# The preparation's ARM tile in two buffers, with other step rates, in a two-layer hybrid backbone

## The chip, the cores and the metric

The kernel runs on one core of a Trainium2 chip. The metric is device time in microseconds (us) from one launch to its end, and the time of a kernel is the median over its runs. The core has a matrix engine (TensorE, PE here), a vector engine (VectorE, DVE), an activation engine (ScalarE, ACT), GpSimd (POOL) and SyncE (SP), which issues nearly all transfers. Each engine works through its own queue in order.

## The reference

1,024 latent tokens and 256 context tokens of width 1,024 go through two layers in float32. Each layer projects the normalised tokens once, splits the columns over four mixers (neighbourhood attention, multi-head latent attention, a bidirectional RWKV-7 recurrence, differential attention), concatenates, projects, and adds a gated MLP with a convolution. Cut to what matters here:

```python
for l in range(DEPTH):
    h_lat = rmsnorm(xl, norm1_g[l]) * (1.0 + sc1) + sh1          # h_ctx alike
    z_lat = jnp.split(h_lat @ w_in[l], IN_SPLITS, axis=-1)       # input projection
    na_l, na_c = na_mixer(z_lat[0], z_ctx[0], rpb[l], need_ctx)
    mla_l, mla_c = mla_mixer(z_lat[1], z_ctx[1], ...)            # low-rank q, k, v, rotary
    rk_l, rk_c = rwkv7_mixer(z_lat[2], z_ctx[2], ...)            # the recurrence
    df_l, df_c = diff_mixer(z_lat[3], z_ctx[3], ...)
    xl = xl + g1 * (jnp.concatenate([na_l, mla_l, rk_l, df_l], axis=-1) @ w_out[l])
    ...                                                          # conv-GLU

def step(S, inp):                                                # rwkv7_scan, per token and head
    r_t, w_t, k_t, v_t, a_t, b_t = inp
    sa = jnp.einsum('bhij,bhj->bhi', S, a_t)
    S = S * w_t[:, :, None, :] + sa[..., None] * b_t[:, :, None, :] + v_t[..., None] * k_t[:, :, None, :]
    return S, jnp.einsum('bhij,bhj->bhi', S, r_t)
```

## The kernel before

The recurrence is not run token by token. The 1,280 tokens are cut into ten slots of 128, and for each slot and direction the kernel prepares matrices with which 64 tokens are one step of a scan (20 steps a layer). That work is spread over the other mixers' work as follows.

In the dense phase of a layer, `main` computes the input projection in groups of six matmuls into a PSUM tile psd (three matmuls per product, of high and low halves: lines 140 to 142). It goes through the RWKV columns, the values, the MLA columns, then the differential and the neighbourhood queries and keys; layer 0 has 1,368 such matmuls. After every group `tick` hands out steps of the side generators: each generator has a rate, its account grows by the rate at each tick, and for every whole 1 in it the generator runs one step (up to its next `yield`) and so emits its instructions. A scheduler then orders each engine's queue by the order of emission and by its own simulation of when operands are ready. So the rates decide how far apart the side work stands in the queues.

- prep (`prep_gen`, lines 283 to about 520) does one slot after the other. partA: matmuls pu (line 333), decays and norms, POOL's kbc (line 368). partB: the tiles BK (DVE) and ARM (POOL, `arm`, lines 402 to 411: per slot four operations of 64x256 at line 407 and eight of 64x128 at line 410). PE multiplies them (`gram`, pg, line 440), ACT and DVE evict into NT, RB and back into ARM (`gout`, lines 446 to 448), PE transposes BK (pbt, line 460), and four transfers write NT, BT, RB and ARM to memory (rnt and rsg). ARM, BT, NT and RB have one buffer each. Slots 2 to 9 wait until the RWKV columns are complete.
- lanes (`lanes_gen`, line 526) inverts small triangular blocks of the slots that prep has written, in three groups: slots 0 and 1, 2 to 5, 6 to 9. A group is a load from rnt, 31 steps of a DVE product and a DVE reduce (lines 547, 548: tiles lpr, lXT, lM), twelve transfers out (lines 554, 557), reloads into the tiles G (lines 567 to 570), and matmuls pmg from G with evictions (lines 580, 582).
- mla (`mla_gen`, line 1390) starts when prep is done and the MLA columns are complete. It keeps its weight halves wq in prep's ARM tile, and its output tiles msp take turns in prep's BT and rwuwa tiles.

After the dense phase comes the attention: scores psL (line 803), softmax (reduces at DVE line 962, exponentials sm_P at ACT line 973), transposes psT, values psV. Beside it run the scan (`rw_step_gen`, line 603: pall at lines 664 and on, loads SG, VS and XB at lines 629 to 631, output tile yt), the modulation vectors (ada) and the recurrence's output stage. The scan's first step may start when the first lanes group is complete, and its later steps as theirs are. The pmg, pall and ada matmuls share one PSUM buffer (tag "R"), so they run in the order in which they are emitted. The yt tile lies in the pool rl, open for the whole mixer.

Of the kernel before, what the change touches and what calls it, by code (L numbers as in the profile page):

```python
# [9 lines left out]
F32 = mybir.dt.float32  # L10
F32R = mybir.dt.float32r
# [6 lines left out]
P = 128  # L18
# [22 lines left out]
class K:  # L41
# [241 lines left out]
    def prep_gen(self, l, rw, pool, psA, psB, F):  # L283
# [111 lines left out]
        def partB(sl):  # L395
            q = st[sl]
            z, kkm, ld, ta, L, E2, kd = (q[k] for k in ("z", "kkm", "ld", "ta", "L", "E2", "kd"))
            Wc = self.Wc[:, sl]
            BK = pool.tile([P, 2, 4, 3, 64], F32, tag="BK", name="BK", bufs=1)
            ARM = pool.tile([P, 2, 2, 4, 2, 64], F32, tag="ARM", name="ARM", bufs=1)  # L400

            def arm(d):
                for e in range(2):
                    r = slice(64 * e, 64 * e + 64)
                    for sl_, a, f in ((0, kkm, ld), (1, z[:, 0], E2)):
                        if d == 0:
                            GT(out=ARM[r, d, e, :, sl_], in0=v4(a)[r], in1=u4(f)[r, d], op=ALU.mult)  # L407
                        else:
# [18 lines left out]
            BKf = BK.rearrange("p d c s t -> p d c (s t)")  # L427
            ARf = ARM.rearrange("p d e c s t -> p d e c (s t)")
            BT = pool.tile([P, 2, 2, 4, 64], F32, tag="BT", name="BT", bufs=1)
# [960 lines left out]
    def mla_gen(self, l, rp, base, pp, ptag, pq, qtag):  # L1390
# [3 lines left out]
        flip = iter(range(10 ** 6))  # L1394

        def big(tag, shape, name, w, dt=F32):
            t = rp.tile([P, w], dt, tag=tag, name=name, bufs=2 if tag in ("sz", "ld", "E2") else 1)
            k = 1
            for x in shape:
                k *= x  # L1400
            t = t[:, :k]
            if len(shape) == 2:
                t = t.rearrange("p (a b) -> p a b", b=shape[1])
            return t
        mv = base.tile([P, 4], F32, name="mlav")
        nc.sync.dma_start(mv, A["mlv"][l])
        U = self.wunits()
        wq = big("ARM", (2, 768), "mwq", 2048, F32R)
        U.add(A["w_uq"][l], 768, lambda: (wq[:, 0], wq[:, 1]))
        U.add(A["w_ukv"][l], 512, lambda: (big("NT", (512,), "mwk", 512, F32R), big("RB", (512,), "mwl", 512, F32R)))  # L1410
        U.dma_to(1)
# [21 lines left out]
            TT(out=tv, in0=tv, in1=rt, op=ALU.add)  # L1433

        def out(t, dst, o):
            sp = big(("BT", "rwuwa")[next(flip) % 2], (2, 512), "msp", 1024, F32R)

            def f1():
                ACT(sp[0:96, 0], t[0:96], AF.Copy)

            def f2():
                TT(out=sp[0:96, 1], in0=t[0:96], in1=sp[0:96, 0].bitcast(F32), op=ALU.subtract)
                for h in range(2):
                    nc.sync.dma_start(dst[h, :, :, o:o + n].rearrange("w r t -> r w t"), sp[0:96, :, h * n:h * n + n].bitcast(F32))
            self.defer(f1, f2)
# [6 lines left out]
        for i, o in enumerate(todo):  # L1452
# [13 lines left out]
            for b in range(nb):  # L1466
                w = slice(b * P, (b + 1) * P)
# [20 lines left out]
            for hp in range(2):  # L1488
# [5 lines left out]
                t = big("ld", (512,), "mt", 512)  # L1494
# [9 lines left out]
                t = big("ld", (512,), "mt", 512)  # L1504
# [5 lines left out]
            for b in range(nb):  # L1510
                w = slice(b * P, (b + 1) * P)
# [119 lines left out]
    def mix(self, l, H, hclose, ada):  # L1631
        nc, A = self.nc, self.A
        need_ctx = l == 0
# [3 lines left out]
        rl, rlclose = self.open("rwl", 1, "right")  # L1637
        rp, rpclose = self.open("rwp", 1, "right")
        psR, prclose = self.open("apr", 1, "right", PSUM)
        psA, c1 = self.open("pA", 2, None, PSUM)  # L1640
        psB, c2 = self.open("pB", 2, None, PSUM)
        F = dict(avail=2, done=0, lanes=0, prep=False)
# [51 lines left out]
        lanes = self.lanes_gen(l, rl, psR, "R", F)  # L1694
        prep = self.prep_gen(l, rw, rp, psA, psB, F)
# [21 lines left out]
        sgp, sgclose = self.open("rsg", 1)  # L1717
        side, n, aclose = self.attn_open(l, [range(q) for q in self.nq[l]], self.lb2, self.POS_M, ("ak", "aw"))
        sp, sclose = self.open("rws", 1)
        adp, adclose = self.open("adw", 1, "right")  # L1720
        F["seg"] = -1
        self.side("scan", self.rw_step_gen(l, sp, sgp, rl, psR, "R", need_ctx, F), self.rates["scan"], scan_done)
        self.side("ada", self.ada_gen(ada, adp, psR, "R"), self.rates["ada"], ada_done)
        alive = True
        while alive or self.sides:
# [23 lines left out]
    bf3 = (3, 4, 3)  # L1749
    lb2 = ((2, (4, 2, 1)),)  # L1750
    lb3 = ((3, (3, 2, 1)),)
    rates = dict(ada=0.2, prep=0.8, lanes=0.5, scan=0.8, mla=1.5, rwo=0.5)

    def wsp(self, o, n):
        a = max(0, min(n, SEQ - o))
# [545 lines left out]
```

## Time and profile before

| what | before |
|---|---|
| median of three runs | 4307.11 us (4297.71 to 4310.25) |
| profiled execution | 4318.05 us, its span 4316.3 us |
| PE, DVE, ACT, POOL busy | 93%, 66%, 46%, 19% of the span |
| mean granted TensorE clock | 0.955 |
| layer 0: dense phase, attention | about 44 to 583, 583 to 1147 us |
| layer 1: dense phase, attention | about 2314 to 2848, 2848 to 3351 us |

The profiled execution lies 10.9 us above the median of the runs. Busy shares are averages over stages; what a stage is limited by is read from its own window. A releaser named beside a wait is what ended last there. PEclk is the share of full clock that TensorE was granted (1.0 is 2.4 GHz, 0.5 is 1.2 GHz).

### The profile page before, as it was taken

To read this page: it belongs to the slowest core of one execution; us is meant where nothing else is said; L and a number is where in the kernel's file an instruction comes from. 1 tells how busy PE (TensorE), PEld (TensorE's weight loads), DVE (VectorE), ACT (ScalarE), POOL (GpSimd) and SP (SyncE) were. 2 spreads that over 40 slices of the span, in tenths; PEclk is the share of its full clock that TensorE was granted. 3 is DMA by queue.
4 is the path that set the end of the run, shared out by engine and by line. 5 is a ranking of instruction groups with operands and counts; after the bars stand their busy time and mean duration, and the time that the engine had idled before them with its cause. 6 is when DMAs were issued, how large, how long until landed. Compare 5 with 4: busy or idle time off the path is not lost. (4 is left out here: it accounts for less than half of the span.)

```text
span 4316.3 us, 76712 instructions
## 1 busy us (share of the span) xinstructions
PE 4027.8 (93%) x29152; PEld 3319.9 (77%) x29152; DVE 2866.8 (66%) x5946; ACT 1982.7 (46%) x4386; POOL 801.9 (19%) x1320
## 2 busy tenths in 40 slices
PE   6999969999999999899998999969999999999998
PEld 4887856677777778788887887856677777788998
DVE  6577686656676765655556667686776766557666
ACT  4444435535554544433334444435545555435443
POOL 3244122212211112000001344122313111111000
PEclk7999979999999999999999999979999999999999
DMA  6444676655523243221213344687636332333332
GB/s 198 151 134 141 204 226 204 224 160 142 151 82 107 78 149 115 71 64 65 64 59 115 137 135 139 204 233 223 206 98 175 104 106 74 125 104 126 94 98 74
DMA packets 423199, 578.40 MB, mean 134 GB/s; under 512 B 109100, under 2 KB 287660, under 8 KB 421296
## 3 DMA queue, kind: packets, MB, share of 16 engines
q1 hardware_dynamic: 422832, 573.51, 42.9%
q8 instruction: 230, 3.77, 0.4%
q14 instruction: 137, 1.12, 0.1%
HBM read 433.47 MB, written 139.92 MB: 133 GB/s over the span
## 5 line engine op out<-in xcount | busy, mean ns | idle before, releaser
L141 PE MATMUL psm<-h_l,whi 128*128 128x512 f32 (+1 forms) x2112 | 710.3, 336 | 9.2 <-DVE h_l L258 9.0
L140 PE MATMUL psm<-h_h,whi 128*128 128x512 f32 (+1 forms) x2112 | 713.5, 338 | 2.3 <-ACT h_h L257 2.3
L142 PE MATMUL psm<-h_h,wlo 128*128 128x512 f32 (+1 forms) x2112 | 709.0, 336 | 0.0
L1888 DVE SCALAR_TENSOR_TENSOR x<-psm,mod,x 128x258 f32<-128x258 f32 (+2 forms) x616 | 327.0, 555 | 288.3 <-PE psm L142 287.9
L973 ACT ACTIVATE sm_P<-psL,sm_n 128x512 f32<-128x512 f32 (+1 forms) x672 | 392.8, 593 | 266.6 <-DVE sm_n L964 238.5
L141 PEld LDWEIGHTS psm<-h_l,whi 128*128 128x128 f32 x2112 | 399.4, 189 | 54.1 <-DVE h_l L258 12.0
L140 PEld LDWEIGHTS psm<-h_h,whi 128*128 128x128 f32 x2112 | 399.4, 189 | 52.0 <-DVE x L1888 4.0
L142 PEld LDWEIGHTS psm<-h_h,wlo 128*128 128x128 f32 x2112 | 399.1, 189 | 43.4 <-issue 0.2
L962 DVE TENSOR_REDUCE sm_m<-psL 128x1 f32<-128x512 f32 (+1 forms) x640 | 353.0, 578 | 88.0 <-PE psL L803 43.3
L140 PE MATMUL psm<-gh,dhi 128*128 128x510 f32 (+3 forms) x1056 | 364.8, 347 | 10.1 <-ACT mb L1852 5.1
L133 ACT ACTIVATE whi<-wst 128x1024 fp32r<-128x1024 f32 x176 | 186.6, 1060 | 401.2 <-PE psm L141 376.7
L141 PE MATMUL psm<-gl,dhi 128*128 128x510 f32 (+3 forms) x1056 | 357.7, 339 | 0.1
L142 PE MATMUL psm<-gh,dlo 128*128 128x510 f32 (+3 forms) x1056 | 357.4, 339 | 0.0
L134 DVE TENSOR_TENSOR wlo<-wst,whi 128x1024 fp32r<-128x1024 f32 x176 | 214.8, 1220 | 169.6 <-ACT whi L133 169.5
L1032 PE MATMUL psV<-PT,V 128*64 128x128 f32 x3488 | 299.3, 283 | 1.2 <-DVE sm_n L964 0.7
L1011 PE MATMUL psT<-ident,sm_P 128*128 128x128 f32 x1744 | 287.3, 287 | 10.6 <-DVE sm_P L1001 6.2
L1032 PEld LDWEIGHTS psV<-PT,V 128*64 128x64 f32 x3488 | 208.8, 137 | 83.7 <-issue 63.7
L1011 PEld LDWEIGHTS psT<-ident,sm_P 128*128 128x128 f32 x1744 | 206.4, 145 | 69.8 <-issue 29.7
L140 PEld LDWEIGHTS psm<-gh,dhi 128*128 128x128 f32 x1056 | 199.6, 189 | 44.6 <-ACT mb L1852 9.3
L142 PEld LDWEIGHTS psm<-gh,dlo 128*128 128x128 f32 x1056 | 200.2, 190 | 21.7
L141 PEld LDWEIGHTS psm<-gl,dhi 128*128 128x128 f32 x1056 | 200.4, 190 | 18.1 <-issue 0.7
L803 PE MATMUL psL<-K,Q 96*128 96x512 f32 (+1 forms) x400 | 148.8, 437 | 68.7 <-DMA Q<-dfq 34.4
(381 smaller groups left out, 9264.7 us busy)
## 6 DMA issues: line engine op xcount, KB each, us to landing
wst<-in_w_up_dram SPq DMA_DIRECT2D x176, 512.0 KB
wst<-in_w_down_dram SPq DMA_DIRECT2D x88, 512.0 KB
adw<-in_ada_w_dram SPq DMA_DIRECT2D x80, 512.0 KB
SG<-rsg SPq DMA_DIRECT2D x40, 896.0 KB
wst<-in_w_out_dram SPq DMA_DIRECT2D x96, 256.0 KB
rsg<-ARM SPq DMA_DIRECT2D x20, 1024.0 KB
K<-dfk SPq DMA_DIRECT2D x16, 960.0 KB
wst<-in_w_rw_dram SPq DMA_DIRECT2D x28, 512.0 KB
```

The lines of the kernel that those rows point to most:

```text
L133: nc.scalar.activation(hi[:, :n], st[:, :n], AF.Copy)
L134: nc.vector.tensor_tensor(out=lo[:, :n], in0=st[:, :n], in1=hi[:, :n].bitcast(F32), op=ALU.subtract)
L140: mm(out, ah, bh, start=first, stop=False)
L141: mm(out, ah, bl, start=False, stop=False)
L142: mm(out, al, bh, start=False, stop=last)
L803: nc.tensor.matmul(ps, ld[0][0:96, j], ld[1][j // 2][0:96, j % 2, o:o + n], start=True, stop=True)
L962: nc.vector.tensor_reduce(out=m[:, j, i:i + 1], in_=src, axis=AX.X, op=ALU.max)
L973: ACT(Pt[:, off:off + n], s["L"][j][t][:, to:to + n], AF.Exp, bias=neg, accum_out=sm[:, j, i:i + 1])
L1011: nc.tensor.transpose(pt[:, j], Ph[:, (bb + j) * P:(bb + j + 1) * P], self.ident)
L1032: nc.tensor.matmul(s["po"][64 * h:64 * h + 64, 0], V[:, kts[i], h], s["PT"][h][:, i], start=i == 0, stop=i == nk - 1, tile_position=(0, 64 ...
L1888: STT(out=x[:, s:e], in0=ps[:, s:e], scalar=mod[:, v, 40 + m:41 + m], in1=x[:, s:e], op0=ALU.mult, op1=ALU.add)
```

## The change

ARM gets a second buffer, in prep and in the mla generator that shares the tag. The new ARM buffer also holds mla's output tile msp, whose two halves take turns. To make room, the scan's output tile yt comes from the pool sp, opened for the attention, instead of rl. The rate of prep goes from 0.8 to 1.3 steps per dense group, and that of lanes from 0.5 to 1.0.

```diff
-            ARM = pool.tile([P, 2, 2, 4, 2, 64], F32, tag="ARM", name="ARM", bufs=1)
+            ARM = pool.tile([P, 2, 2, 4, 2, 64], F32, tag="ARM", name="ARM", bufs=2)
...
-            t = rp.tile([P, w], dt, tag=tag, name=name, bufs=2 if tag in ("sz", "ld", "E2") else 1)
+            t = rp.tile([P, w], dt, tag=tag, name=name, bufs=2 if tag in ("sz", "ld", "E2", "ARM") else 1)
...
         wq = big("ARM", (2, 768), "mwq", 2048, F32R)
+        msp = big("ARM", (4, 512), "msp", 2048, F32R)
...
-            sp = big(("BT", "rwuwa")[next(flip) % 2], (2, 512), "msp", 1024, F32R)
+            i = 2 * (next(flip) % 2)
+            sp = msp[:, i:i + 2]
...
-        self.side("scan", self.rw_step_gen(l, sp, sgp, rl, psR, "R", need_ctx, F), self.rates["scan"], scan_done)
+        self.side("scan", self.rw_step_gen(l, sp, sgp, sp, psR, "R", need_ctx, F), self.rates["scan"], scan_done)
...
-    rates = dict(ada=0.2, prep=0.8, lanes=0.5, scan=0.8, mla=1.5, rwo=0.5)
+    rates = dict(ada=0.2, prep=1.3, lanes=1.0, scan=0.8, mla=1.5, rwo=0.5)
```

The count of instructions on each engine stays the same; their order changes. In layer 0's PE queue the eight late slots begin behind 568 to 1,110 psd matmuls before (slot 2 to slot 9), and behind 569 to 974 now; prep's last matmul stands behind 1,117 and 1,023, mla's first behind 1,131 and 1,023. Three places in the queues show the rest.

POOL's queue in the preparation of a middle slot of layer 0 (krs, kbc: norms; Wc, zvr: small copies; ARM from kkm and ld, and from sz and E). Before:

```order
L359 TENSOR_TENSOR krs<-krs,mhalf 128x4
L368 COPY kbc<-krs 128x256
L381 COPY Wc<-E_2211 128x4
L381 COPY Wc<-E_2211 128x2x2
L336 COPY zvr<-sz 128x2x128
L407 TENSOR_TENSOR ARM<-kkm,ld 64x4x64
L407 TENSOR_TENSOR ARM<-sz,E_2211 64x4x64
...
L410 TENSOR_TENSOR ARM<-kkm,ld 64x2x64 x2
L410 TENSOR_TENSOR ARM<-sz,E_2211 64x2x64 x2
```

Now:

```order
L359 TENSOR_TENSOR krs<-krs,mhalf 128x4
L368 COPY kbc<-krs 128x256
L381 COPY Wc<-E_2238 128x4
L381 COPY Wc<-E_2238 128x2x2
L407 TENSOR_TENSOR ARM<-sz,E_2238 64x4x64 x2
L410 TENSOR_TENSOR ARM<-sz,E_2238 64x2x64 x4
L336 COPY zvr<-sz 128x2x128
L407 TENSOR_TENSOR ARM<-kkm,ld 64x4x64 x2
L410 TENSOR_TENSOR ARM<-kkm,ld 64x2x64 x4
```

The half of ARM that comes from sz and E moves ahead, before the next slot's zvr, since no earlier reader of the tile holds it back; the other half stays behind kbc.

PE's queue at the start of layer 0's attention (psL scores, psT transposes, psV values, adaps the modulation, pmg the lanes' matmuls, pall the scan). Before:

```order
L1011 MATMUL psT<-ident,sm_P 128x128 x10
L1032 MATMUL psV<-PT,V 64x128
L803 MATMUL psL<-K,Q 128x512
L803 MATMUL psL<-K,Q 128x256
L803 MATMUL psL<-K,Q 128x512 x2
...
L664 MATMUL pall<-VS,SG 64x64 x4
...
L676 MATMUL pall<-Dt,XB 64x64 x8
L1556 MATMUL adaps<-adw,sc_60 32x256 x4
```

Now:

```order
L1032 MATMUL psV<-PT,V 64x128
...
L803 MATMUL psL<-K,Q 128x256
L803 MATMUL psL<-K,Q 128x512
L580 MATMUL pmg<-G_5296,G_5297 32x32 x32
...
L1558 MATMUL adaps<-adw,sc_60 32x256 x4
L1011 MATMUL psT<-ident,sm_P 128x128 x4
L580 MATMUL pmg<-G_5296,G_5297 32x32 x16
...
L582 MATMUL pmg<-G_5296,G_5297 32x32 x16
...
L664 MATMUL pall<-VS,SG 64x64 x8
```

The pmg matmuls of the third lanes group, which stood behind 85 to 99 score matmuls, now stand behind 22 to 34 of them; the scan's first pall moves from behind 18 to behind 39. In layer 1 pmg moves from behind 78 to 94 to behind 12 to 19, and the first pall stays (18 and 19). On DVE the group's 31 steps, of which 23 stood among the first softmax reduces (up to the 22nd), all stand ahead of the first reduce now, in both layers.

SP's queue at the same place (Q, K, V: the attention's loads; SG, VS, XB: the scan's; msk, nb: mask and bias; rxf, ry: the lanes' outputs; G: their reloads). Before:

```order
L630 DMA SG<-rsg 128x1792 x4
L799 DMA Q<-dfq 96x4x128
L879 DMA V<-vtm 128x10x128
...
L816 DMA K<-mlk 96x2x1280 x2
...
L847 DMA msk<-in_na_mask_dram 128x512
L850 DMA nb<-in_rpbp_dram 128x2x512 x2
L629 DMA VS<-rvt 64x2x128 x2
L631 DMA XB<-rxf 128x256
```

Now:

```order
L799 DMA Q<-dfq 96x4x128
L1446 DMA mlq<-msp 96x2x256
L879 DMA V<-vtm 128x10x128
L557 DMA rxf<-lXT 16x32x32
L554 DMA ry_91<-lX 512x1x32
...
L570 DMA G_5297<-rnt 32x8x128 x2
...
L816 DMA K<-mlk 96x2x1280 x2
...
L567 DMA G_5296<-ry_91 32x8x128
L569 DMA G_5296<-rxf 32x8x32 x4
```

The third lanes group's twelve outputs and its two loads from rnt now stand ahead of the third Q and the first mla K, and the ten other loads of G stand ahead of the last XB, behind the mask, the bias and most of VS and XB. In layer 1 the G loads come right behind the first Q, ahead of the second.

## Rows read from the trace of the kernel before

**Rows 1.** Windows: us, PE, PEld, DVE, ACT, POOL busy, PEclk, DMA share, GB/s

```profile
196.00:285.00 89.00, 83.55 (x653) 77.62 (x651) 78.43 (x137) 36.99 (x79) 32.83 (x45) 0.96 0.37 116
380.00:443.00 63.00, 56.91 (x308) 47.05 (x309) 57.63 (x99) 26.20 (x62) 28.78 (x32) 0.89 0.40 138
443.00:583.00 140.00, 134.17 (x1015) 116.28 (x1014) 94.27 (x186) 68.02 (x130) 28.22 (x29) 0.98 0.65 194
583.00:640.00 57.00, 22.65 (x101) 13.39 (x100) 52.60 (x101) 17.35 (x50) 12.38 (x22) 0.51 0.95 288
715.00:757.00 42.00, 41.28 (x520) 31.59 (x520) 24.37 (x61) 21.94 (x61) 4.42 (x12) 0.82 0.54 174
2848.00:2905.00 57.00, 24.65 (x140) 15.02 (x140) 52.32 (x103) 16.07 (x48) 12.18 (x20) 0.52 0.93 280
2957.00:3003.00 46.00, 45.04 (x631) 33.90 (x631) 28.13 (x73) 25.40 (x72) 5.66 (x12) 0.96 0.73 225
```

**Rows 2.** PE's waits 110:590, waiting line, releaser: us, times, longest

```profile
PE pg L440 <- POOL ARM L407: 8.6, 5, 4.1
PE pkb L378 <- POOL kbc L368: 4.0, 2, 3.0
```

**Rows 3.** PE's waits, layer 1's dense phase, 2376:2852

```profile
PE pg L440 <- POOL ARM L407: 9.8, 5, 4.1
PE pkb L378 <- POOL kbc L368: 4.1, 2, 2.9
```

**Rows 4.** POOL's waits 196:490

```profile
POOL ARM L407 <- DMA rsg<-ARM: 64.8, 6, 19.6
POOL ARM L407 <- DVE lXT L548: 9.9, 1, 9.9
```

**Rows 5.** PE's timeline, layer 0: start us, us, instruction, count, idle before

```profile
209.47 1.51 PE L333 MATMUL pu<-szm,rwuwa 33*128 33x128 f32 x16 [0.72 <-DMA szm<-rzm]
...
404.76 1.59 PE L333 MATMUL pu<-szm,rwuwa 33*128 33x128 f32 x9
...
627.16 0.87 PE L664 MATMUL pall<-VS,SG 128*64 128x64 f32 x8 [2.47 <-issue]
...
638.41 1.01 PE L803 MATMUL psL<-K,Q 96*128 96x256 f32 x2
...
726.08 1.19 PE L580 MATMUL pmg<-G,G 32*32 32x32 f32 x32
```

**Rows 6.** DVE by line, 588:650: busy us, mean ns, idle before

```profile
L547 DVE TENSOR_TENSOR lpr<-lXT,lM 128x81 f32<-128x81 f32 (+22 forms) x23 | 21.7, 942 | 0.4
L548 DVE TENSOR_REDUCE lXT<-lpr 128x8 f32<-128x64 f32 (+23 forms) x24 | 14.3, 597 | 0.4
L962 DVE TENSOR_REDUCE sm_m<-psL 128x1 f32<-128x512 f32 (+1 forms) x22 | 12.5, 600 | 2.9 <-PE psL L803 2.9
```

**Rows 7.** PE's waits 583:640

```profile
PE psL L803 <- ACT sm_P L973: 13.8, 5, 4.0
PE psL L803 <- DMA Q<-dfq: 13.0, 1, 13.0
```

**Rows 8.** POOL's operations on ARM, whole span: min/median/max ns, first and last start

```profile
L410 POOL TENSOR_TENSOR ARM<-kkm,ld x80: 446/460/4042, 137.5 to 2724.3; 64x128 f32<-64x128 f32 x80
...
L407 POOL TENSOR_TENSOR ARM<-kkm,ld x40: 717/838/6682, 135.7 to 2717.3; 64x256 f32<-64x256 f32 x40
```

**Rows 9.** POOL's timeline, two of a slot's ARM operations

```profile
410.33 6.68 POOL L407 TENSOR_TENSOR ARM<-kkm,ld 64x256 f32<-64x256 f32 x1 [14.63 <-DMA rsg<-ARM]
...
419.30 4.46 POOL L410 TENSOR_TENSOR ARM<-kkm,ld 64x128 f32<-64x128 f32 x2
```

**Rows 10.** SP's timeline, the last XB of the attention's start

```profile
629.44 0.59 SPq L631 DMA_DIRECT2D XB<-rxf  x1
```

**Rows 11.** SP's issues of lanes outputs and G loads: min/median/max ns

```profile
L557 SPq DMA_DIRECT2D rxf<-lXT x48: 278/572/2485, 267.4 to 2927.8; - x48
...
L569 SPq DMA_DIRECT2D G<-rxf x48: 302/456/2353, 279.6 to 2942.2; - x48
```

## The prediction

> **What bounds the kernel now.** I read the busy times by stage first, then what TensorE (PE) waits for in the stages where it idles, then what those releasers wait for themselves. PE is busy 93% of the span, so time can be won only where PE stands still. By stage [rows 1] it stands still 5.5 of 89 us, 6.1 of 63 and 5.8 of 140 in three stretches of layer 0's dense phase, and 34.4 of 57 us at the start of the attention (583 to 640), where the granted clock falls to 0.51, about the 1.2 GHz level. Layer 1 has the same hole: 32.4 of 57 us at 0.52.
>
> In the dense phase PE waits for the preparation's gram inputs: 8.6 us in layer 0 and 9.8 in layer 1 for ARM, 4.0 and 4.1 for kbc, which stands behind ARM's operations on POOL [rows 2, 3]. That is 8.6 + 9.8 + 4.0 + 4.1 = 26.5 us in all. POOL is late because its first ARM operation of a slot waits for the transfer of the previous slot's ARM out of the only buffer: 64.8 us in six waits in layer 0 alone, and once 9.9 us for VectorE (DVE) [rows 4]. So a slot starts every 27.9 us: slot 2's first pu matmul is at 209.47, slot 9's at 404.76, seven slots later [rows 5].
>
> At the start of the attention the DVE is the busy engine (52.6 of 57 us). There it works off the third lanes group, 21.7 + 14.3 = 36.0 us, between the softmax's reduces [rows 6]; layer 1's DVE is 52.3 of 57 us busy there [rows 1]. PE waits 13.8 us for the exponentials that depend on those reduces, and 13.0 us for the transfer of the first Q [rows 7].
>
> **The change part by part.** The instruction counts are the same on every engine; the edit moves instructions, lifts one wait and shifts transfers. It has three priced terms.
>
> *A, the second ARM buffer.* The 64.8 us of POOL's waiting for rsg<-ARM [rows 4] goes. PE gets back at most the 26.5 us above. It won't get all: RB, NT and BT keep one buffer, so the evictions of the next slot still wait for that slot's transfers, only one step later in the slot; and the preparation is now asked for faster. In the new order slot 2 starts behind 569 matmuls of the dense phase and slot 9 behind 974, against 568 and 1,110 before: 58 instead of 77 per slot, so the cadence wanted is 27.9 x 58/77 = 21 us. POOL's ARM work of a slot is four large and eight small operations; at their minima that is 4 x 0.72 + 8 x 0.45 = 6.5 us [rows 8], well inside 21. I take -5 per layer, a little under half of the 13 per layer that is there, because the releaser in line behind the transfer is the DVE: that shows already once for 9.9 us [rows 4], and the DVE is 78.4 of 89 and 57.6 of 63 us busy in these stretches [rows 1]. Bounds: -26.5 if all waits go, and +39.1 if each of the eight slots costs PE the longest wait of rows 2 in both layers (8 x 4.1 x 2 = 65.6, less 26.5).
>
> Beside a busy DVE the same ARM operation took 6.68 us instead of 0.72, and two small ones 4.46 us instead of 0.9 [rows 8, 9]. The four large ones of that slot took 419.30 - 410.33 = 9.0 us where 2.9 would do. The Trainium skill, page "SBUF — State Buffer", section "Who interferes with whom", says that a VectorE instruction with two SBUF inputs and a GpSimd instruction that reads SBUF exclude each other, whoever issues first holding the shared ports for the whole instruction. The lanes' multiplication is such an instruction, the rows agree, and the rule speaks against this change: it pulls two-input DVE work and POOL's ARM work closer together. By the rule alone A would come out as a loss (the second rival); by the waits of rows 2 and 3 it is a gain.
>
> *T, the dense phase's tail.* The lanes group that ran under the softmax now ends ahead of its first reduce, so its 36 us stand in the tail. There the DVE is busy 94.3 of 140 us between 443 and 583 [rows 1]; with 36 more it is 130.3, or 93%. The work fits, which is why I cost it as friction and not as 36 us: at 88% DVE in 196 to 285 PE stood still 6.1% of the time, at 91% in 380 to 443 9.7% (ARM waits within), against 4.2% in the tail. So 140 us would lose between 8.6 and 13.5 us instead of 5.8: +2.8 to +7.7 per layer. I take +3, the row without the ARM wait's share, and keep 0 and +7.7 as ends. Two layers: +6.
>
> *B, the start of the attention.* Without the lanes' 36 us the DVE needs 52.6 - 36.0 = 16.6 us of the 57, so the waits for exponentials (13.8 us, and about as much in layer 1, where lanes and hole have the same size) can go; the 13.0 us for Q can't. Relief is up to -14 per layer. What is late next: the matmuls of the third lanes group (pmg). They stood far behind the scan's first steps (the scan's first pall ran at 627, the first such pmg at 726 [rows 5]); now they stand ahead of the scan, after 22 score matmuls in layer 0, and they need the group's reloads G. The queue on SP gives their time: the issue of the last XB ended at 630.0, 47 us after the dense end at 583 [rows 10]; the lanes' 12 outputs and two loads of NT are put ahead of it, 14 x 0.57 = 8.0 us, and the ten other G loads stand just before that XB, 10 x 0.46 = 4.6 us [rows 11]. So G is asked for by 583 + 47 + 12.6 = 643. PE, now at the 22nd score matmul at 638.8 (the second of the two from 638.41 [rows 5]), could be there at 625 and would then stand 18 us, which takes the 13.8 back and 4 more. PE's queue is in order: behind the waiting pmg stand all scores, transposes and the scan. The lanes' outputs also push the third Q and the first mla K back by 8 us, which makes it 12. What speaks for a gain is that the DVE is free behind the wait and the scores kept back find no queue there. Bounds -14 and +12; I take -3, a little below their middle. In layer 1 the G loads stand ahead of the second Q and pmg after 12 to 19 scores, with no 47 us of other transfers ahead; I take -8 (bounds -21, the 34.4 us of idle less the 13.0 for Q, and +8 for the queue). Sum -11.
>
> *At nothing.* The stretch where pmg ran inside the scan (715 to 757 and 2957 to 3003) has PE busy 41.3 of 42 and 45.0 of 46 us [rows 1]: the matmuls are only done elsewhere, and the scan that paused there still ends before the attention does. If that cover were gone it would be the 0.7 + 1.0 us left idle. The tile msp used two tiles in turn, BT and rwuwa, and now two halves of one: two buffers either way, and no wait of rows 2 and 3 is for either. The tile yt moves pool and keeps its two buffers and instructions.
>
> Sum on the profiled execution: 4318.05 - 10 + 6 - 11 = 4303. That execution lies 10.9 us above the median of 4307.11, so the median expected is 4303 - 10.9 = 4292, a gain of 15 us or 0.35%.
>
> **The rivals.**
>
> *Full relief.* All of A and the two exponential waits go and the tail swallows the lanes: -26.5 - 2 x 13.8 = -54.1, so 4264 for the profiled execution and 4253 for the median. For it: the POOL waits are long and regular, and the lanes fit into the tail by sum. Against it: G's late loads in layer 0, and the DVE's 88 to 93%.
>
> *Slower, POOL starved.* The place is POOL's ARM chain in the dense phase. With the DVE's lanes steps twice as dense (one per dense group instead of half), each of the eight late slots loses as the slot at 410 did. By rows 9 four large operations take 9.0 us and eight small ones at 2.23 us take 17.8, together 26.8, more than the 21 us of cadence. Then PE waits the 4.1 us of rows 2 for every slot: +39.1 with B's -11 left, so 4318 + 28 - 10.9 = 4335. It decides from where the ARM operations of a slot exceed some 17 us, since POOL has about 4 us of other work in one (32.8 us busy for 89/27.9 = 3.2 slots in 196 to 285 [rows 1], or 10.3 a slot, less ARM's 6.5). For it: rows 9 and the DVE's share. Against it: the second buffer lets POOL run a slot early, and the median large operation of forty is 0.84 us [rows 8], so most are not hit.
>
> *No change.* The ARM wait comes back as the wait of RB, NT and BT for their transfers, and the start of the attention waits for G instead of the exponentials: between +0 and -8, so about 4303. For it: one buffer of three tiles that go out in the same burst. Against it: these are asked for later in a slot than ARM.
>
> *The change doesn't do what it says.* The tile would still wait for the old transfer. That the order shows POOL's operations regrouped speaks against it.
>
> **How the numbers follow.** Forecast 0.40, with its own range of 4280 to 4303; full relief 0.22; slower 0.20; no change 0.16; the change without effect 0.02. This kernel's measurement tells a change from none at about 0.3%, 13 us: faster is below 4294, slower above 4320. Faster: 0.23 of the forecast, all of full relief, 0.02 of no change: 0.47. Slower: the slower rival and 0.01 of no change: 0.21, and 0.01 more of the forecast's tail: 0.22. Same: the rest, 0.31. The range of 4250 to 4325 leaves out a third of full relief (0.07) and two thirds of the slower case (0.13).
>
> **What the changed profile would show.** A: no wait of ARM for rsg<-ARM on POOL; a slot every 21 us, slot 9's pu near 357 instead of 404.76; PE's waits for ARM and kbc under 8 us a layer. If the ARM operations of a slot take over 17 us from slot 5 on, the slower rival is right. T: between 443 and 583 the DVE at about 93% and PE's idle share near 6%; a wait of the dense evictions above 8 us makes T wrong. B: no lanes multiplication after the first softmax reduce; PE's waits for the exponentials gone; a new wait of pmg for G in layer 0 of 5 to 15 us. If PE passes pmg without one, B is too small by about 11; if PE idles more than 34 us between the last dense matmul and 57 us behind it, B has the wrong sign. The prediction as a whole is wrong if the second buffer only moves the wait to RB or BT with the same 26 us.

## The result and the profile after

The changed kernel takes 4343.15 us, the median of six runs (4332.27 to 4349.38), against 4310.38 us for six runs of the kernel before: ratio 1.0072, 95% interval 1.0048 to 1.0095. It is slower by 0.7%, where 4292 us and a gain of 0.35% were forecast, and it lies outside the range of 4250 to 4325. Its profiled execution took 4345.60 us, its span 4343.5.

Where the time went shows between marks of PE's own queue: the first and last dense matmul (psd) of a layer, then score matmuls (psL) by their number. The table holds the differences of their start times in the two profiled executions.

| us | dense phase | to score 100 | to score 540 | to score 600 | to the layer's end | layer |
|---|---|---|---|---|---|---|
| layer 0 before | 536 | 172 | 352 | 89 | 1121 | 2270 |
| layer 0 changed | 539 | 184 | 338 | 114 | 1122 | 2297 |
| layer 1 before | 530 | 160 | 328 | 198 | 778 | 1994 |
| layer 1 changed | 531 | 170 | 322 | 197 | 776 | 1995 |

The end of layer 1 is PE's last matmul. In these two executions all of the loss but 3 us lies in layer 0's attention. The dense phase is as long as before in spite of the second buffer. Score 540 of layer 0 comes at 1104 us before and at 1105 now; the stretch behind it is 25 us longer. Next come windows of the changed kernel, with the columns of [rows 1]: stretches from there, then 640 to 715, then two that are bounded by score numbers (0 to 100, 540 to 600):

```profile
196.00:285.00 89.00, 83.97 (x623) 79.21 (x622) 75.47 (x138) 36.23 (x80) 44.65 (x62) 0.88 0.34 107
380.00:443.00 63.00, 57.43 (x315) 44.95 (x313) 58.27 (x88) 23.40 (x52) 15.98 (x23) 0.92 0.42 119
443.00:583.00 140.00, 132.33 (x994) 116.74 (x995) 107.33 (x211) 65.74 (x127) 15.21 (x16) 0.93 0.62 192
583.00:640.00 57.00, 17.49 (x45) 10.27 (x43) 36.91 (x72) 17.21 (x48) 7.32 (x11) 0.52 0.85 235
640.00:715.00 75.00, 62.42 (x664) 45.44 (x664) 28.90 (x70) 30.75 (x83) 14.14 (x26) 0.63 0.51 152
...
606.60:768.00 161.40, 126.83 (x1355) 89.87 (x1356) 83.63 (x208) 72.45 (x210) 29.77 (x65) 0.72 0.69 204
1105.00:1219.00 114.00, 97.90 (x627) 76.09 (x626) 64.15 (x173) 55.07 (x140) 15.91 (x18) 0.90 0.44 129
```

The last three answer to these of the kernel before:

```profile
640.00:715.00 75.00, 64.18 (x859) 45.33 (x857) 52.56 (x121) 38.25 (x114) 27.10 (x52) 0.94 0.74 209
...
596.30:753.00 156.70, 123.78 (x1460) 86.87 (x1461) 114.47 (x243) 73.08 (x213) 40.12 (x74) 0.79 0.75 225
1105.00:1194.00 89.00, 85.85 (x579) 65.91 (x577) 59.95 (x159) 52.95 (x136) 11.30 (x11) 0.98 0.52 150
```

Read the busy time and the clock together: between 640 and 715 PE is busy 62 and 64 of 75 us in both, but at a granted clock of 0.63 it gets through 664 matmuls, at 0.94 through 859 (the mix of shapes is not the same, so the counts are only a rough measure). DVE has become free there (28.9 us against 52.6), as meant; PE did not get faster by it. In 443 to 583 DVE rises from 94.3 [rows 1] to 107.3 us.

PE's waits in the dense phase (110 to 583), which answer to [rows 2], and behind them POOL's for ARM (196 to 490), which answer to [rows 4]; line, releaser, us in total, times, longest:

```profile
PE pg L440 <- ACT BT L464: 6.7, 2, 4.8
PE pbt L460 <- DVE ARM L448: 6.3, 5, 2.7
PE pkb L378 <- POOL kbc L368: 3.0, 1, 3.0
```

```profile
POOL ARM L407 <- ACT kkm L389: 2.5, 2, 1.9
POOL ARM L407 <- DMA rsg<-ARM: 2.2, 1, 2.2
```

The 64.8 us of POOL's waiting are 2.2 now, and PE no longer waits for POOL's ARM; in its place stand ACT's eviction of BT and DVE's of ARM. At the start of the attention (583 to 720) PE's waits, which answer to [rows 7], are:

```profile
PE pmg L580 <- DMA G<-ry: 19.6, 1, 19.6
PE psL L803 <- DMA Q<-dfq: 16.9, 1, 16.9
PE psL L803 <- ACT sm_P L973: 8.5, 5, 2.1
```

In the same window the kernel before has 14.3 us for the exponentials and 20.9 us in two waits for Q. The wait for the exponentials is smaller by 6 us, the first wait for Q is longer (16.9 for 13.0 us), and a stop of 19.6 us is new. From the last dense matmul to the first score there are 23.3 us instead of 15.7. SP's timeline shows what stood ahead of the reloads: the lanes' outputs, Q, mask, bias and scan loads. PE's timeline follows, then two windows behind the stop (start us, us, instruction; columns as above):

```profile
612.79 3.53 SPq L557 DMA_DIRECT2D rxf<-lXT  x1
...
625.33 1.53 SPq L570 DMA_DIRECT2D G<-rnt  x2
...
635.76 3.86 SPq L629 DMA_DIRECT2D VS<-rvt  x2
...
647.33 0.59 SPq L567 DMA_DIRECT2D G<-ry  x1
647.97 1.93 SPq L569 DMA_DIRECT2D G<-rxf  x4
```

```profile
649.99 1.91 PE L580 MATMUL pmg<-G,G 32*32 32x32 f32 x32 [19.61 <-DMA G<-ry]
...
694.57 0.88 PE L664 MATMUL pall<-VS,SG 128*64 128x64 f32 x16
```

```profile
650.00:690.00 40.00, 37.41 (x377) 28.16 (x377) 13.36 (x30) 18.53 (x48) 5.07 (x6) 0.50 0.45 134
...
700.00:720.00 20.00, 20.00 (x280) 14.74 (x276) 14.21 (x38) 10.59 (x32) 7.30 (x19) 1.00 0.48 146
```

The clock was at half already before the stop (0.52 over 583 to 640), as in the kernel before (0.51 [rows 1]). Now it stays there up to about 695; in the kernel before it was back at about 643. The scan's first pall moved from 627 [rows 5] to 695. The output stage of the recurrence now ends at 1146 instead of 1117 in layer 0, and PE waits behind it (PE's waits, 1100 to 1290):

```profile
PE pso L140 <- ACT h_h L1778: 8.9, 1, 8.9
PE psL L803 <- DMA Q<-dfq: 5.4, 1, 5.4
```

SP's queue shows the way (its wait between 1125 and 1160, then its timeline): the store of the output stage's last tile (oy to ymix) waits 14.1 us for DVE, and behind it stand the output projection's loads h_l and the next scores' K.

```profile
SPq L784 <- DVE oy L783: 14.1, 1, 14.1
```

```profile
1155.11 4.40 SPq L1777 DMA_DIRECT2D h_l<-ymix  x8
1159.55 1.15 SPq L796 DMA_DIRECT2D K<-dfk  x2
```

Before, the first of h_l and that K were issued at 1143.58 and 1126.08:

```profile
1126.08 0.96 SPq L796 DMA_DIRECT2D K<-dfk  x2
...
1143.58 3.00 SPq L1775 DMA_DIRECT2D h_l<-ymix  x5
```

### The profile page after: what moved, and what is told of

Its sections match the earlier page's. It is cut to its first block, busy times and chain, and to the rows that moved or that the text cites. A ratio compares the mean times of both kernels' runs of the same rounds, so it can differ in the third digit from the quotient of the medians.

```text
span 4343.5 us, 76655 instructions
## 1 busy us (share of the span) xinstructions
PE 4032.6 (93%) x29152; PEld 3331.2 (77%) x29152; DVE 2869.2 (66%) x5946; ACT 1979.9 (46%) x4386; POOL 796.0 (18%) x1320
## 3 DMA queue, kind: packets, MB, share of 16 engines
q1 hardware_dynamic: 422832, 573.51, 43.5%
## 5 line engine op out<-in xcount | busy, mean ns | idle before, releaser
L1032 PEld LDWEIGHTS psV<-PT,V 128*64 128x64 f32 x3488 | 211.8, 140 | 86.6 <-issue 64.2
L1021 ACT ACTIVATE PT<-psT 128x512 f32<-128x512 f32 (+2 forms) x300 | 152.1, 525 | 127.9 <-PE psT L1011 126.7
```

What stands on the lines that cost most here:

```text
L1021: ACT(dst, src, AF.Copy)
L1032: nc.tensor.matmul(s["po"][64 * h:64 * h + 64, 0], V[:, kts[i], h], s["PT"][h][:, i], start=i == 0, stop=i == nk - 1, tile_position=(0, 64 ...
```

## The experiments

Each ratio is taken against runs of the kernel before that were timed along with it; marks and waits are those of one profiled execution. The first four take the change apart: buffer, prep's rate, lanes' rate.

**The buffer alone**, with msp and yt where the change put them: 4277.80 us (4272.40 to 4288.55), ratio 0.9944 (0.9927 to 0.9962).

```diff
-    rates = dict(ada=0.2, prep=1.3, lanes=1.0, scan=0.8, mla=1.5, rwo=0.5)
+    rates = dict(ada=0.2, prep=0.8, lanes=0.5, scan=0.8, mla=1.5, rwo=0.5)
```

> The changed kernel with the old rates (prep 0.8, lanes 0.5): second ARM buffer, msp in it, yt in the other pool, nothing else. Theory S (the loss comes from the third lanes group's pmg matmuls standing ahead of layer 0's scan in the one shared PSUM buffer, so that the scan, and behind it the recurrence's output stage, end some 30 us later than before and the output projection waits): here pmg stands behind 62 to 85 score matmuls and the scan's first pall behind 4, so the loss is gone: 0.995 to 1.000 of before, with the output stage ending at 1117 or earlier. Rival D (the loss comes from the 36 us of lanes work on DVE in the dense tail): gone as well. Rival P (the second buffer itself, POOL's ARM work beside a busy DVE, or the moved tiles cost): 1.003 to 1.007.

The loss is gone and a gain of 24 us stands in its place, a little more than theories S and D had expected. PE's waits in its dense phase (110 to 568, then layer 1, 2350 to 2815):

```profile
PE pkb L378 <- POOL kbc L368: 9.8, 3, 6.1
...
PE pg L440 <- POOL ARM L407: 1.2, 1, 1.2
```

```profile
PE pkb L378 <- POOL kbc L368: 11.1, 3, 6.1
```

The ARM wait fell from 8.6 us [rows 2] to 1.2, and in layer 1 it is gone (9.8 [rows 3]). The wait for kbc rose from 8.1 to 20.9 us in the two layers. The dense phases take 524 and 521 us (536 and 530 before); mla ends earlier (562 instead of 583) and the scan's loads begin to be issued inside the dense phase's tail: the first pall runs at 587. Rival P is out. Windows of the two dense phases, this kernel first, then the kernel before:

```profile
45.20:568.90 523.70, 489.56 (x3334) 416.58 (x3334) 395.05 (x717) 257.90 (x522) 184.65 (x261) 0.95 0.52 164
2288.40:2809.20 520.80, 490.21 (x3322) 417.93 (x3322) 371.96 (x720) 247.36 (x518) 162.59 (x252) 0.94 0.49 154
```

```profile
44.40:580.60 536.20, 496.55 (x3328) 420.52 (x3328) 384.17 (x695) 255.29 (x516) 178.43 (x252) 0.94 0.49 156
2314.20:2844.60 530.40, 494.71 (x3315) 420.30 (x3316) 366.66 (x701) 244.81 (x513) 161.13 (x244) 0.94 0.46 148
```

PE stands still 5 us less in each (34.1 and 30.6 instead of 39.7 and 35.7) and is busy 7.0 and 4.5 us less with practically the same matmuls.

**Prep's rate on top** (lanes back at 0.5): 4292.23 us (4285.53 to 4300.41), ratio 0.9968 (0.9957 to 0.9979).

```diff
-    rates = dict(ada=0.2, prep=1.3, lanes=1.0, scan=0.8, mla=1.5, rwo=0.5)
+    rates = dict(ada=0.2, prep=1.3, lanes=0.5, scan=0.8, mla=1.5, rwo=0.5)
```

> The changed kernel with lanes back at 0.5 and prep at 1.3. pmg stands behind 55 to 91 scores, the scan behind 4. Theory S: 0.994 to 1.001 of before. Rival D: the third lanes group still starts 100 psd matmuls earlier than before, so part of its DVE work lies in the tail: 1.002 to 1.004. Rival P: 1.004 to 1.008, with PE waits in the dense phase longer than the 12.6 us (layer 0) of before.

The time lies in theory S's range, so D and P fall; yet prep's rate gives back 0.24% of the buffer's 0.56. Its dense phases are 536 and 537 us, 12 and 16 longer than with the buffer alone. One stretch shows how (windows, buffer alone first, then with prep's rate):

```profile
196.00:300.00 104.00, 101.60 (x753) 93.56 (x752) 86.12 (x157) 45.48 (x99) 43.48 (x69) 0.93 0.42 134
```

```profile
196.00:300.00 104.00, 93.66 (x719) 88.16 (x718) 84.81 (x160) 45.58 (x99) 54.71 (x77) 0.88 0.38 120
```

PE idles 10.3 instead of 2.4 us, at a lower clock, and POOL is busier (54.7 against 43.5). The named waits there are one of 4.6 us for the first lanes group's G, one of 3.0 for kbc and one of 2.3 for BT; what makes them come with the rate was not separated.

**Lanes' rate on top of the buffer** (prep at 0.8): 4340.79 us (4338.14 to 4347.63), ratio 1.0086 (1.0067 to 1.0104).

```diff
-    rates = dict(ada=0.2, prep=1.3, lanes=1.0, scan=0.8, mla=1.5, rwo=0.5)
+    rates = dict(ada=0.2, prep=0.8, lanes=1.0, scan=0.8, mla=1.5, rwo=0.5)
```

> The changed kernel with prep back at 0.8 and lanes at 1.0. pmg stands behind 4 to 16 scores, ahead of the scan (16). Theory S: the lanes chain starts as late as before (near 576), so PE stands at pmg until its reloads come, some 40 us into the attention, and the scan starts behind it: 1.004 to 1.012 of before. Rival D: little lanes work is in the dense tail, which ends as before; only the start loses: 0.998 to 1.002. Rival P: 1.000 to 1.003.

Theory S's numbers came out, by the stop it named. PE's longest wait, 568 to 720:

```profile
PE pmg L580 <- DMA G<-ry: 43.3, 1, 43.3
```

In layer 1 PE stops there for 42.1 us. So lanes' rate costs 1.4% with prep at 0.8 (1.0086 against 0.9944) and 1.0% with prep at 1.3 (1.0072 against 0.9968). The dense phases, 528 and 522 us, are nearly those of the buffer alone, which speaks against D; the attention's start (to score 100) is longer by 35 us in layer 0 and 33 in layer 1, less than the stop, and nothing comes on top at the end: scores 540 to 600 take 89 us in layer 0.

**The rates without the buffer**: the kernel before with both new rates. 4348.55 us (4341.38 to 4357.34), ratio 1.0093 (1.0075 to 1.0111).

```diff
-    rates = dict(ada=0.2, prep=0.8, lanes=0.5, scan=0.8, mla=1.5, rwo=0.5)
+    rates = dict(ada=0.2, prep=1.3, lanes=1.0, scan=0.8, mla=1.5, rwo=0.5)
```

> The kernel before with both new rates (prep 1.3, lanes 1.0) and one ARM buffer. Seen so far: the second buffer alone gains 0.56%, prep's rate takes 0.24 of it back, lanes' rate alone costs 1.4 against the buffer alone. If the buffer's gain is independent of the rates, this is the changed kernel plus 0.56%: 1.011 to 1.014 of before. If one buffer holds the preparation back by itself, so that the higher rate has no grip, the third lanes group comes later and pmg stands behind 12 to 25 scores: 1.005 to 1.009. The ARM wait on POOL should be back, 60 us or more in layer 0's dense phase.

This lies just above the second range. At the new rates the buffer is worth about 0.2%, which the intervals do not resolve, against 0.56% at the old ones. Of the expected wait for the transfer only 16.0 us were left; POOL's queue waited for other producers (24.8 us once for BK), so that part of the expectation failed. This kernel loses elsewhere than the changed one: at the start of layer 0's attention PE stops at pmg for 0.8 us only, but the dense phases take 549 and 547 us (536 and 530 before) and scores 540 to 600 are longer by 12 us in layer 0 and 21 in layer 1. Why the dense phases grow was not taken apart.

**The scan ahead of pmg.** 4340.00 us (4333.10 to 4354.74), ratio 1.0086 (1.0068 to 1.0104).

```diff
+            while l == 0 and s0 == 6 and F.get("seg", -9) < 1:
+                yield
             for first in (True, False):
```

> The changed kernel, with one condition more: in layer 0 the third lanes group issues its pmg matmuls only when the scan has done two segments (four steps). Rates, buffers and the DVE work stay as changed; pall now stands behind 19 scores and pmg behind 85 to 94. Theory S: the scan starts near 635 to 650 instead of 695, the 19.6 us wait of pmg for G is gone, and the time comes back to 0.999 to 1.003 of before. Rival D: the dense tail and its DVE work are unchanged, so 1.005 to 1.008, as the changed kernel. A third outcome, that the scan starts early but is held up in its middle by the late pmg and the output stage still ends at the attention's end, gives 1.003 to 1.007 and the time is then set by where the output stage ends, not by where the scan starts.

Theory S as it stood falls: the order was turned round and nothing came back. PE's timeline has the reason:

```profile
649.34 0.88 PE L666 MATMUL pall<-VS,SG 128*64 128x64 f32 x7 [18.10 <-issue]
```

The scan stops PE until the same moment, 649. The view names no releaser; that it is the scan's own loads is read from SP's timeline, where VS stands behind the lanes' outputs too and is issued from 639:

```profile
639.21 4.03 SPq L631 DMA_DIRECT2D VS<-rvt  x2
```

**The scan held behind pmg in the kernel before.** 4318.28 us (4306.15 to 4334.40), ratio 1.0015 (1.0001 to 1.0029).

```diff
-        while F["lanes"] <= need(0):
+        while F["lanes"] <= (9 if l == 0 else need(0)):
```

> The kernel before with layer 0's scan held until the third lanes group is complete: pall stands behind 58 to 370 scores instead of 18 to about 270, the output stage behind 390 to 584. The dense phase and the entry to the attention stay as before. Theory R (what counts is when the shared PSUM buffer gets its first work, from there it takes about 493 us whatever the order: 489 to 496 us in all six kernels so far): the buffer still starts near 635 with the modulation's matmuls, so the output stage ends near 1130 and the time is 1.000 to 1.004 of before. Theory S (what counts is when the scan starts): the scan starts some 70 us later, the output stage ends after the attention, and the stretch from score 540 to score 600 takes 25 us or more longer than the 89 of before: 1.006 to 1.015.

The first pall ran at 693, as late as in the changed kernel, scores 540 to 600 took 131 us instead of 89, and still it cost only 0.15%: with the scan out of the way score 540 came 22 us earlier than before (1082 for 1104), score 600 20 us later, and the layer ended 4 us later. PE had other work while the scan was held. Theory S's stretch came true, its time did not. Nor did R hold to the letter: the shared buffer took 526 us, not 493.

**Half the turns of the shared buffer**, on the changed kernel: 4332.24 us (4324.32 to 4338.60), 1.0050 (1.0034 to 1.0065). On the buffer-only kernel: 4291.07 us (4282.68 to 4295.76), 0.9955 (0.9939 to 0.9970).

```diff
-    adg = 1
+    adg = 2
```

> The changed kernel with two modulation products to one PSUM tile instead of one (half as many turns of the shared buffer, 32 fewer, and half the evictions; same matmuls). Theory R: at some 3 us a turn the buffer's work shrinks from 496 to about 400 us, the output stage no longer ends last, the stretch from score 540 to 600 falls from 114 to near 90 us: 1.001 to 1.004 of before. Theory S: the output stage ends where it does now because the scan starts at 695 and has its own chain of 20 steps; only a few us change: 1.005 to 1.008.

> The second buffer with the old rates (0.8, 0.5) and the same halving of the modulation's turns. Theory R: layer 0 is held by the shared buffer there too (its end and the next layer's start lie 1,206 us apart, 1,195 to 1,199 in the others), so 0.988 to 0.993 of before. If PE's work in the attention is the bound there (10 us idle of 185 in scores 100 to 300), it is the buffer-only kernel's 0.993 to 0.996.

The buffer's occupation fell by 12 us, not 96, scores 540 to 600 still took 115 us, and the buffer-only kernel gained nothing. The second lies in the range that was given for PE's work as the bound. Theory R is out: the shared PSUM buffer is not the bound.

**The third lanes group late**, in the changed kernel: 4304.68 us (4294.66 to 4312.75), ratio 0.9985 (0.9974 to 0.9996).

```diff
-            while F["done"] < s0 + ns:
+            while F["done"] < s0 + ns or (s0 == 6 and F.get("seg") is None):
```

> The changed kernel with the third lanes group held back until the attention opens (both layers), so its 36 us of DVE steps stand beside the softmax again as before the change; both rates, both buffers and groups one and two as changed. Theory T (the loss is the lanes chain in the dense tail: mla's steps share DVE with it and end at 589 instead of 561, so everything that is loaded once mla's tiles are free, the scan's VS and XB among it, is late, and the shared PSUM buffer starts at 650 instead of 599): mla ends near 561, the buffer starts near 600 and the time is 0.995 to 0.999 of before, like the 0.9968 of lanes at 0.5. Rival G (what costs is that PE's in-order queue stops at pmg for its reloads G, wherever the chain runs): pmg stands behind 39 scores instead of 22 and its wait goes on: 1.002 to 1.007.

Most of the loss is gone, though mla still ends late (582 instead of the 561 with lanes at 0.5), which theory T did not expect. The wait for G is no longer among PE's waits (583 to 760):

```profile
PE psL L803 <- DMA Q<-dfq: 18.8, 1, 18.8
PE adaps L1558 <- DMA adw<-in_ada_w_dram: 12.9, 2, 7.9
PE pall L664 <- DMA SG<-rsg: 2.5, 2, 2.2
```

**The same with prep at 0.8**: 4315.09 us (4306.40 to 4322.24), ratio 1.0013 (0.9998 to 1.0027).

```diff
-    rates = dict(ada=0.2, prep=1.3, lanes=1.0, scan=0.8, mla=1.5, rwo=0.5)
+    rates = dict(ada=0.2, prep=0.8, lanes=1.0, scan=0.8, mla=1.5, rwo=0.5)
```

> The second buffer with lanes at 1.0 and prep at 0.8 (1.0086 in the earlier run, where PE stood 43 us at pmg in layer 0) and the third lanes group held back until the attention opens. pmg stands behind 48 to 78 scores instead of 4 to 16. Theory G: the 43 us stop is gone in both layers and the time is 0.994 to 0.999 of before. Theory T: mla and the scan's loads are still late (VS and XB stand behind mask, bias and the lanes' outputs here): 0.999 to 1.004.

Against 1.0086 the stop of 43 us is gone, but one of 19.1 us has come at pall, where T expected one for the scan's loads (the view names no releaser), and one of 16.9 us for the exponentials.

**The third chain cut short** (28 of 31 steps left out in each layer): 4278.16 us (4270.44 to 4286.33), ratio 0.9921 (0.9903 to 0.9938).

```diff
             for t in range(1, 32):
+                if s0 == 6 and t > 3:
+                    yield
+                    continue
```

> The changed kernel with the third lanes group's chain cut to 3 of its 31 steps (28 products and reduces on DVE are left out in each layer; its transfers and pmg stay). Theory T: the dense tail is free of the 36 us, mla ends near 560, pmg runs inside the dense phase, and the loss turns into a gain: 0.985 to 0.994 of before, in both layers. Rival P (prep's higher rate and POOL beside DVE are what costs): 0.999 to 1.004.

All of the loss and more is gone, in both layers (2249 and 1975 us), as theory T expected. It takes away the DVE work and the late pmg at once, so it does not separate them.

**No reloads** (the third lanes group's ten reloads of G and two loads from rnt are left out; POOL clears the tiles): 4306.93 us (4301.62 to 4316.93), ratio 0.9997 (0.9984 to 1.0010).

```diff
+                if s0 == 6:
+                    nc.gpsimd.memset(G1[64 * e:64 * e + 64, :nj], 0.0)
+                    nc.gpsimd.memset(G2[a, :nj], 0.0)
+                    continue
                 nc.sync.dma_start(w2(G1[a]), y1[e])
```

> The changed kernel with the third lanes group's ten reloads of G and two loads from rnt left out in both layers (POOL clears the tiles instead), so that pmg has nothing to wait for from memory; the DVE chain stays in the dense tail and the outputs stay where the change put them. pmg stands behind 8 to 19 scores, the scan behind 19. Theory G (the price of lanes' rate is PE's stop at pmg for G, and the half clock behind it): the 19.6 us wait goes, scores 0 to 100 of layer 0 take about 142 us instead of 161, the output stage is not last, and the time is 0.998 to 1.002 of before. Theory T (the chain in the tail makes mla late, and with it all transfers of the attention's start): PE stops at the scan's first matmul for VS or XB instead, some 15 us, and the time is 1.003 to 1.007.

This is theory G's time: by the ratios 32 us are back. mla ends at 589 and the lanes chain lies in the tail, as in the changed kernel, and yet the profiled execution is 36 us shorter, all in layer 0 (2297 to 2261 us); scores 540 to 600 are at 88 again. The stop is not gone, as theory G had it. PE's waits (583 to 760) keep a shorter one, for POOL's clearing behind the chain, and it ends at 627 instead of 650:

```profile
PE psL L807 <- DMA Q<-dfq: 17.2, 1, 17.2
PE pmg L584 <- POOL G L568: 12.8, 1, 12.8
```

Layer 1, where the wait for G was 5.8 us, did not change (1995 us). The missing transfers also free SP's queue, but what stands behind them comes little earlier: the scan's first VS is issued at 634.57 instead of 635.76 and the modulation's weights (adw) at 647.29 instead of 653.68. The scan's first pall runs at 660 instead of 695, and the clock is back at about 660.

**Prep at 1.0 and 0.65** with the buffer and lanes at 0.5: 4288.67 us (4273.77 to 4305.63), 0.9947 (0.9927 to 0.9968), and 4291.72 us (4287.40 to 4308.10), 0.9957 (0.9941 to 0.9973).

```diff
-    rates = dict(ada=0.2, prep=1.3, lanes=1.0, scan=0.8, mla=1.5, rwo=0.5)
+    rates = dict(ada=0.2, prep=1.0, lanes=0.5, scan=0.8, mla=1.5, rwo=0.5)    # and prep=0.65
```

> The second buffer with lanes at 0.5 and prep at 1.0, between the two runs at 0.8 (0.9944) and 1.3 (0.9968). If the loss with prep's rate grows evenly with it, 0.995 to 0.996; if it comes from the clock falling at a crowd of waits in one stretch, as likely on either side: 0.993 to 0.997.

> The second buffer with lanes at 0.5 and prep at 0.65. If less crowding helps further: 0.991 to 0.994. If mla and the third lanes group get too late, so that the scan's loads stand behind mask and bias again: 0.996 to 1.002.

Neither differs from 0.8 by more than the intervals; 0.65 fell between its two ranges. At 0.65 the dense phases fall to 504 and 494 us, but mla then runs on after them and the first score waits 55 us, where 15 were usual. Of the kernels that do all the work, the buffer with the old rates has the lowest time (0.9944); prep at 1.0 (0.9947) cannot be told from it.

## Why the prediction was wrong

**A, the second buffer: right in sign, its size by other means than its working.** The prediction took -10 of at most -26.5, the sum of PE's waits for ARM and kbc. The buffer alone measured 0.56%, some 24 us, which is nearly that bound, but this fit is luck. Of the 26.5 us 22.1 are still there: PE's waits for POOL's ARM fell from 18.4 us to 1.2, as meant, and those for kbc rose from 8.1 to 20.9. The 22 us by which its two dense phases are shorter are about half PE's idle time (11 us) and half busy time with the same matmuls (11.5 us), in layer 0 at a slightly higher clock (0.95 for 0.94). These parts are rough: the two profiled executions lie 46 us apart, the medians 27. Which of the moved operations brings that was not separated. DVE, named as the next releaser in line, hardly held ARM up (POOL's other waits for ARM: 12.1 us in eight waits on kkm, an ACT operation, in the buffer-only kernel, hidden, since PE's wait was 1.2). What took the gain away again in the dense phase was prep's rate, which the working had as a cadence (21 us forecast; 22 measured, slot 9's pu at 364 instead of 357) but not as a price: 0.24%.

**The starved POOL, the rival on the slower side, did not happen.** The slowest large ARM operation took 4.6 us instead of 6.7 [rows 8], the median from kkm 0.77, and among PE's waits POOL's ARM no longer appears. The time came out near that rival's 4335 (which leaves out T's +6) by another way. The rule of the Trainium skill weighed there (page "SBUF — State Buffer", section "Who interferes with whom": a VectorE instruction with two SBUF inputs contends with a GpSimd instruction that reads SBUF) may hold for single operations; no run here shows it as a loss.

**T, the tail: about right in size, for less work than it reckoned.** It took +3 a layer. Lanes' rate changed the dense phases by +4 and +1 us with prep at 0.8 and by +3 and -6 with prep at 1.3. DVE rose to 107, not 130 us, of 140: the lanes took 31.3 us of it where they had taken 11.5 before (three of the 31 steps ran only behind 583), and mla and prep took 6 us less.

**B, the start of the attention, with the attention's end put at nothing: the step that failed.** The stop itself was foreseen (18 us at pmg for G in layer 0, 19.6 measured) and so was its cause, SP's queue; that the length fits so well is partly luck, since both of its ends came later than worked out (PE was there at 630 instead of 625, G at 650 instead of 643). The step priced it as the 18 us less the 13.8 us of exponentials relieved, put +12 as the upper end and took -3. In layer 0 the way to score 100 became 12 us longer. The prediction's own sign for B had shown it: PE stands still 39.5 of the 57 us from 583 to 640 in layer 0 (57.0 - 17.5), more than the 34 it named. What was wrong:

- The relief in the exponentials was 5 to 6 us, not 13.8. A second wait for Q of 7.9 us went as well, but the first, which the step held fixed, grew: the first score came 7 to 8 us later behind the dense phase, in both layers.
- Behind the stop PE stayed at half clock up to 695 (643 before), and the sum has nothing for that. Over scores 0 to 100 the clock is 0.72; it was 0.79 before, and with lanes at 0.5 it is 0.86 (line below). As an estimate from busy time and mean clock, 126.8 us x 0.28 = 35 us of full-clock work is lost there, against 123.8 x 0.21 = 26 before and 121.3 x 0.14 = 17 with lanes at 0.5.
- The layer's end became longer. The part at nothing says that the scan still ends before the attention does. It does (its last pall runs at 969), but the output stage behind it now ends only as the attention's last matmuls run: 41 us behind score 540 (13 before). Its last store holds SP's queue, and scores 540 to 600 take 25 us more, in which PE stands 16 us instead of 3 (114.0 - 97.9 and 89.0 - 85.9). Over the runs this stretch goes with that lag: 13 us of lag and 88 or 89 us before and with lanes at 0.5, in the third group late and without reloads; 41 us and 116 with the scan ahead of pmg; 71 us and 131 with the scan held.

```profile
597.60:740.00 142.40, 121.28 (x1526) 87.53 (x1526) 92.51 (x219) 74.27 (x216) 36.23 (x75) 0.86 0.81 232
```

Between scores 100 and 540 the changed kernel makes up 14 us on the kernel before, so the start and the end together show as 24 us in the table. Against lanes at 0.5 it makes up nothing: 24 us more to score 100, 25 more from 540 to 600. By the ratios lanes' rate costs 45 us with prep at 1.3 (0.0104 x 4310), where T and B together forecast a gain of 5. Leaving out the reloads gives back 32 of them (1.0072 to 0.9997): PE passes pmg 23 us earlier, the clock comes back 35 us earlier, and the output stage no longer ends late. In layer 1 the forecast of -8 met a stop of 5.8 us, a start 10 us longer, and the layer came out even.

**At nothing, the scan's place: small by itself.** Holding the scan 66 us costs 0.15%, and pulling it ahead of pmg gains nothing, because PE then stops for the scan. In these runs it did not matter much where in the attention the scan stood; it mattered whether PE had anything to do while its queue waited.

**What stays open.** Whether the price of lanes' rate is PE's stop alone: without the reloads the stop is shorter and earlier, not gone, and SP's queue is 1 to 6 us ahead. Why the rates cost as much with one ARM buffer, where PE does not stop at pmg. And what keeps the changed kernel's layer 1 equal to the one before with its longer start.

## What to carry to other kernels

A stop of an in-order queue is to be priced with what follows it, and its length alone is a poor guide: here the rate that brought a stop of 19.6 us cost about twice that, through the clock and through the work that came out at the stage's end, while with prep at 0.8 stops of 43 us cost 34 us a layer. Look up which chain ends last in the stage, and what stands behind its last transfer in the issuing queue. Before work is pulled ahead on one engine, look up where its transfers then stand in the queue that issues them: work that arrives early but waits for a late transfer blocks everything behind it. And a change that moves several rates with a buffer is best taken apart first; here the buffer gained 0.56% and the rates on top of it lost 1.3.

## What was not expected of the hardware

Busy time hid the loss. In the 75 us from 640 PE was busy 62.4 us, before 64.2, but at 0.63 of the clock it did 664 matmuls and at 0.94 it did 859. The level stayed down although PE was busy: between 650 and 690 it was granted half clock throughout while it was busy 37.4 of 40 us.
